# Split weights of the second layer stored for the second sequence, and stores issued one chunk later

## The chip, the cores and the metric

One Trainium2 chip, one core of it. The time is device microseconds (us) of one execution; a time is the median of the runs shown. The profile is one further execution of the same program, and all rows below are from it.

## What is computed

Two independent sequences (`x_prompt`, `x_sample`), each of 16 meta tokens and 512 tokens (528 columns, `T`), go through the same two layers with the same weights:

```
def _trunk(x, ...):
    h = concatenate([meta, x], axis=1)
    h = h + gdn_mixer(rmsnorm(h, ln_g[0]), gdn_w_in, ..., gdn_w_out)     # layer 1
    h = h + mla_mixer(rmsnorm(h, ln_g[1]), mla_w_in, mla_w_uq, mla_w_ukv, ..., mla_w_out)   # layer 2
    return h[:, 16:]
```

Layer 1 is a gated DeltaNet in both directions (8 heads); layer 2 is attention over low-rank projections (16 heads): `cq` and `ckv` are normed projections of the layer's input, q comes from `cq @ w_uq`, k and v from `ckv @ w_ukv`, a rotary part is added, and softmax(q k) v is multiplied by silu of a gate z and projected by `mla_w_out`.

## The kernel before

**Products in two halves.** Every float32 factor x of a projection is kept as a high half `xh` (x cast to float32r) and a low half `xl` = x - `xh`, and a product is three matmuls (`mm3`, L75 to L77): high by high, high by low, low by high. A weight matrix is used in chunks of 4 blocks of 128 rows and 128 columns (256 KB; `wh` and `wl` are the halves of a chunk). Some chunks of layer 2 have 2 blocks and 128 columns (128 KB).

**`weights()`** (L204) prepares chunks. It loads the raw chunk into `wraw` (SP issues the DMA, L218), ScalarE (ACT) casts it into `wh` (L219), and GpSimd (POOL) subtracts, `wl = wraw - wh` (L220, recorded as L88). Each of `wraw`, `wh` and `wl` has three buffers. With `s=0` the two halves are also stored to device memory (`wc`, L222 to L224), and with `s=1` nothing is split: SP loads both halves from `wc` (L211 to L213). Before the change only layer 1 passes `s`: its 98 chunks are split and stored with the first sequence and loaded with the second. The 94 chunks that layer 2 uses of `mla_w_in`, `mla_w_uq` and `mla_w_ukv` are split anew for each sequence, and so are the output projections' chunks, which are used by one sequence at a time and pass no `s`.

**Stages.** `run()` (L1129) emits layer 1 for the first sequence, layer 1 for the second, and then layer 2 in the same way. The output projections (`out_proj`) and the preparations of the next stage (`l2_prep`) are woven in. Layer 2 works on pairs of heads, 8 pairs a sequence. A pair's head (`head(u)`) takes ten chunks in this order: `pair_k` (two, k of both heads), `pair_qrope` (one, the rotary part of q), `pair_q` (one, first head), `pair_v` (one), `pair_q` (second head), `pair_z` (two for each head). It runs beside the attention (`pair_scores`, `pair_out`) of the pair before it.

**The chain inside a pair.** `pair_k` makes the scales of k: `rk` goes out to device memory (`rkd`, L998) and comes back on all partitions as `rs` (L955, 528 KB). `pair_qrope` projects and sends `qg` to `sw` with its quarters swapped, in four DMAs (`swap`, L840, shown as `acc<-acc`). POOL then multiplies (L956, L957), VectorE (DVE) adds (L964) and makes the low half `RL` of the rotary part (two instructions, L970), ACT its high half `SQ` (L968, then a DMA to the other partitions, L969). In the attention DVE takes the maximum `mx` of a score tile (L1089), ACT the exponential into `P` (L1093), DVE scales `P` (L1096), and TensorE (PE) transposes it (L1108, L1110) and multiplies by v. The 0.5 KB rows of `pst` (L1113, L1114) are the meta tokens' share. The gated output of a head, `zs`, is written to `y2` (L1127).

**What sets the order.** Each engine runs its own list of instructions in order. The lists come from the Tile scheduler, which orders the traced instructions by a simulated timeline and puts in the semaphores; `behind()` forces a few orders. All DMAs are issued by SP, one list as well: a DMA whose wait isn't over holds up those behind it.

Of the kernel before, what the change touches and what calls it, by code (L numbers as in the profile page):

```python
# [8 lines left out]
F32 = mybir.dt.float32  # L9
# [14 lines left out]
class Trunk:  # L24
    def __init__(self, ctx, tc, ins, outs):
        self.tc, self.nc, self.ins, self.outs = tc, tc.nc, ins, outs
        self.ctx = ctx
        self.cn = ctx.enter_context(tc.tile_pool(name="cn", bufs=1))
        self.dr = ctx.enter_context(tc.tile_pool(name="dr", space=DRAM, bufs=1))
        self.sa = ctx.enter_context(tc.tile_pool(name="sa", bufs=1, reuse_waits="tile"))  # L30
        self.n = 0
        self.inner = None
        self.cached = {}
        self.last_sc = self.last_P = None
        self.next_pool(self.BUFS1, self.PBUFS1)

# [167 lines left out]
    def weights(self, parts, kt, width=128, hk=4, s=None):  # L204
        nc = self.nc
        res = []
        key = None if s is None else (parts[0][1].tensor.name, parts[0][1].offset)
        for k0 in range(0, kt, hk):
            wh = self.t("wh", [128, hk, width], F32R)
            wl = self.t("wl", [128, hk, width], F32R)  # L210
            if s == 1:  # L211
                for t, c in zip((wh, wl), self.cached[key, k0]):
                    nc.sync.dma_start(t.rearrange("p k c -> p (k c)").bitcast(F32), c)  # L213
            else:
                raw = self.t("wraw", [128, hk, width])
                for off, ap in parts:
                    w = ap.shape[1]
                    nc.sync.dma_start(raw[:, :, off:off + w], ap[128 * k0:128 * (k0 + hk)].rearrange("(k p) c -> p k c", p=128))  # L218
                nc.scalar.copy(wh, raw)  # L219
                self.last_wl = self.sub(nc.gpsimd, wl, raw, wh)  # L220
                if s == 0:
                    self.cached[key, k0] = cs = [self.d("wc", [128, hk * width]) for _ in range(2)]  # L222
                    for t, c in zip((wh, wl), cs):
                        nc.sync.dma_start(c, t.rearrange("p k c -> p (k c)").bitcast(F32))  # L224
            for k in range(hk):
                res.append((wh[:, k], wl[:, k]))
        return res

    def project(self, w, rhs, kt, c0, n, tag="pj", m=128):
        ps = self.p(tag, [m, n])  # L230
# [617 lines left out]
    def l2_prep(self, s, hd, rsd, out):  # L848
        nc = self.nc
        V, A, G, PE = nc.vector, nc.scalar, nc.gpsimd, nc.tensor  # L850
        W = self.ins["mla_w_in"][0]
# [13 lines left out]
        ckv = oh, ol = self.t("ckvH", [128, 2, T], F32R), self.t("ckvL", [128, 2, T], F32R)  # L865
        pss = [self.p(t, [128, 264]) for t in ("x", "tr")]
        for j in range(2):
            w = self.weights([(0, W[:, 512 + 128 * j:640 + 128 * j])], 8)
            for c, c0 in enumerate(KC):
                cs = slice(c0, c0 + 264)  # L870
                ps = self.project(w, hn, 8, c0, 264)
                A.copy(oh[:, j, cs], ps)
                self.sub(V, ol[:, j, cs], ps, oh[:, j, cs])
                sq = self.t("raw", [128, 264])
                A.activation(sq, ps, AF.Square)
                self.colsum(pss[c], self.split("sq", sq, [128, 264]), 0, 264, j == 0, j == 1)
# [8 lines left out]
            A.copy(oh[:, j], x)  # L885
            self.sub(V, ol[:, j], x, oh[:, j])
        yield
        w = self.weights([(0, W[:, 768:832]), (64, W[:, 768:832])], 8)
        kpg = self.t("acc", [128, T])
        sqpe = self.t("raw", [64, T])  # L890
        for c0 in KC:
# [15 lines left out]
        cq = self.t("cqH", [128, 4, 512], F32R), self.t("cqL", [128, 4, 512], F32R)  # L907
        sm = self.t("sqr", [128, 512])
        for j in range(4):
            w = self.weights([(0, W[:, 128 * j:128 * j + 128])], 8)  # L910
            ps = self.project(w, hn, 8, NM, 512)
            gj = self.cqg[:, j:j + 1]
            A.activation(cq[0][:, j], ps, AF.Copy, scale=gj)
# [27 lines left out]
    def pair_qrope(self, u):  # L941
        nc = self.nc
        V, A, G, PE = nc.vector, nc.scalar, nc.gpsimd, nc.tensor
        UQ, cq, hs = self.ins["mla_w_uq"][0], u["c"]["cq"], u["hs"]
        w = self.weights([(64 * j, UQ[:, 192 * h + 128:192 * h + 192]) for j, h in enumerate(hs)], 4)
        ps = self.project(w, cq, 4, 0, 512)
        qg = self.t("acc", [128, 512])
        A.activation(qg, ps, AF.Copy, scale=self.qrg)
# [24 lines left out]
    def pair_k(self, u):  # L973
        nc = self.nc
# [5 lines left out]
        kk = self.t("sqH", [128, T])  # L980
        sq = self.t("raw", [128, T])
        for j, h in enumerate(hs):
            w = self.weights([(0, UKV[:, 256 * h:256 * h + 128])], 2, hk=2)
            for c0 in KC:
                ps = self.project(w, ckv, 2, c0, 264)
                A.copy(kr[:, j, c0:c0 + 264], ps)
            o, nn = self.SIDES[j]
            A.activation(kk[o], kr[nn, j], AF.Square)
            A.activation(sq[o], kr[o, j], AF.Square)
            G.tensor_tensor(kk[o], kk[o], sq[o], op=ALU.add)  # L990
# [9 lines left out]
    def pair_q(self, u, j):  # L1000
# [1 line left out]
        V, A, G, PE = nc.vector, nc.scalar, nc.gpsimd, nc.tensor  # L1002
        UQ, cq, sqr, h = self.ins["mla_w_uq"][0], u["c"]["cq"], u["sqr"], u["hs"][j]
        o = self.SIDES[j][0]
        w = self.weights([(0, UQ[:, 192 * h:192 * h + 128])], 4)
        ps = self.project(w, cq, 4, 0, 512)
        qH = self.t("qH", [128, 512], F32R)
        qL = self.t("qL", [128, 512], F32R)
# [18 lines left out]
    def pair_v(self, u):  # L1027
        nc = self.nc
        V, A, G, PE = nc.vector, nc.scalar, nc.gpsimd, nc.tensor
        UKV, ckv, hs, hp = self.ins["mla_w_ukv"][0], u["c"]["ckv"], u["hs"], u["hp"]  # L1030
        w = self.weights([(128 * j, UKV[:, 256 * h + 128:256 * h + 256]) for j, h in enumerate(hs)], 2, width=256, hk=2)
        VH, VL = self.V2[hp % 2, 0], self.V2[hp % 2, 1]
        for tp in range(2):
            ps = self.p("pj", [128, 2, 256])
# [29 lines left out]
    def pair_z(self, u, j):  # L1064
        nc = self.nc
        V, A, G, PE = nc.vector, nc.scalar, nc.gpsimd, nc.tensor
        W, hn, h = self.ins["mla_w_in"][0], u["c"]["hn"], u["hs"][j]
        w = self.weights([(0, W[:, 832 + 128 * h:960 + 128 * h])], 8)
        ps = self.project(w, hn, 8, NM, 512)
        zs = u["zs"][j] = self.t("zs", [128, 512])  # L1070
        A.activation(zs, ps, AF.Tanh, scale=0.5)
# [260 lines left out]
```

## Time and profile before

| | |
|---|---|
| time, median of 3 runs | 2630.35 us (2624.48 to 2631.34) |
| profiled execution, its own time | 2632.01 us |
| its span, first to last instruction | 2630.3 us |
| PE busy | 2468.7 us, 94% |
| DVE busy | 1732.9 us, 66% |
| ACT busy | 1408.4 us, 54% |
| POOL busy | 1166.6 us, 44% |
| granted TensorE clock, mean | 0.97 |

Layer 1 takes the first 1340 us or so, layer 2 the rest; its first sequence's attention runs to about 1920 us, the second's preparation and attention from there to about 2390 us, and an output projection ends the program. In rows, the number after `x` is a count, and what stands after `|` or in brackets is idle time of the engine before the instruction with what ended it. A line such as L88 is that of a helper: the names of the tiles tell what is worked on.

### The profile page before, as it was taken

The page shows a single profiled execution, that of the slowest core. Times are in us where ns is not written, and L with a number is a line of the kernel's source. Part 1 is how long each engine was busy: PE and PEld are TensorE (multiplying, and loading weights), DVE is VectorE, ACT ScalarE, POOL GpSimd, SP SyncE. Part 2 cuts the span into 40 slices and gives each one's busy share as a digit, 9 for nine tenths or more (in the row PEclk, how much of TensorE's full clock was granted, in tenths as well). Part 3 has the DMA queues.
Part 4 walks back from the last instruction along what each step waited for, and adds up shares of the span by engine and source line. Part 5 has one row for each costly group of instructions (what it writes and reads, how often), then busy time and mean ns, then how long its engine had stood idle before and what let it go on. Part 6 is the DMA issues. An engine that isn't in the chain of part 4 may idle for free.

```text
span 2630.3 us, 52159 instructions
## 1 busy us (share of the span) xinstructions
PE 2468.7 (94%) x19083; PEld 2212.1 (84%) x19083; DVE 1732.9 (66%) x3915; ACT 1408.4 (54%) x3424; POOL 1166.6 (44%) x1157
## 2 busy tenths in 40 slices
PE   8889999998999999999989889998998989999999
PEld 7878888888888889888989878888887878888787
DVE  6987888777788867786454256667775567666421
ACT  5545655545455554545545365666656556665432
POOL 6544545432433323323445454555535544554343
PEclk9999999988999999999999999999999999999999
DMA  6544545442333354444465422233332223225575
GB/s 206 176 121 136 153 128 164 136 138 86 112 91 90 113 172 138 133 122 144 127 213 167 130 79 71 73 72 83 90 89 74 81 70 69 77 69 153 167 222 148
DMA packets 453216, 321.06 MB, mean 122 GB/s; under 512 B 134812, under 2 KB 364430, under 8 KB 452960
## 3 DMA queue, kind: packets, MB, share of 16 engines
q1 hardware_dynamic: 452960, 317.73, 41.9%
q8 instruction: 150, 2.46, 0.4%
q14 instruction: 106, 0.87, 0.1%
HBM read 216.02 MB, written 92.67 MB: 117 GB/s over the span
## 4 chain that ended last, share of the span: by engine, by line
PE 58%; DVE 20%; DMA 8%; ACT 6%; issue 4%; POOL 2%; SPq 2%; ACTq 0%; POOLq 0%; DVEq 0%
PE pj L75 12%; PE pj L76 12%; PE pj L77 12%; PE ch L692 2%; PE po L710 2%; DVE acc L374 2%; DVE RL L88 2%; DMA acc<-acc 2%; DVE Yt L504 1%; DVE kq L374 1%; PE ch L703 1%; DVE Y L506 1%; PE lv L552 1%; PE tr L1110 1%; DMA T<-Td 1%
## 5 line engine op out<-in xcount | busy, mean ns | idle before, releaser
L88 POOL TENSOR_TENSOR wl<-wraw,wh 128x512 fp32r<-128x512 f32 (+2 forms) x414 | 547.6, 1325 | 708.8 <-ACT wh L219 675.3
L75 PE MATMUL pj<-hnH,wh 128*128 128x264 f32 (+4 forms) x2080 | 632.8, 305 | 18.9 <-ACT wh L219 5.2
L77 PE MATMUL pj<-hnH,wl 128*128 128x264 f32 (+3 forms) x2080 | 627.6, 303 | 2.6 <-POOL wl L88 1.9
L76 PE MATMUL pj<-hnL,wh 128*128 128x264 f32 (+3 forms) x2080 | 625.2, 301 | 0.7 <-DVE hnL L784 0.6
L219 ACT CAST wh<-wraw 128x512 fp32r<-128x512 f32 (+2 forms) x414 | 248.2, 600 | 346.0 <-PE pj L76 195.8
L75 PEld LDWEIGHTS pj<-hnH,wh 128*128 128x128 f32 (+1 forms) x2080 | 398.9, 192 | 37.6 <-ACT wh L219 5.7
L77 PEld LDWEIGHTS pj<-hnH,wl 128*128 128x128 f32 (+1 forms) x2080 | 398.3, 192 | 17.8 <-POOL wl L88 3.3
L76 PEld LDWEIGHTS pj<-hnL,wh 128*128 128x128 f32 (+1 forms) x2080 | 399.0, 192 | 15.8 <-issue 2.5
L76 PE MATMUL pj<-h2L,wh 128*128 128x512 f32 (+1 forms) x544 | 205.5, 378 | 3.2 <-DVE h2L L88 3.1
L77 PE MATMUL pj<-h2H,wl 128*128 128x512 f32 (+1 forms) x544 | 205.8, 379 | 0.0
L75 PE MATMUL pj<-h2H,wh 128*128 128x512 f32 (+1 forms) x544 | 205.4, 379 | 0.3
L1089 DVE TENSOR_REDUCE mx<-S 128x1 f32<-128x528 f32 x128 | 89.9, 703 | 66.3 <-PE S L1086 65.5
L1093 ACT ACTIVATE P<-S,mx,qs 128x528 f32<-128x528 f32 x128 | 101.5, 793 | 46.6 <-DVE mx L1090 42.7
L76 PEld LDWEIGHTS pj<-h2L,wh 128*128 128x128 f32 x544 | 102.5, 188 | 22.4 <-DVE h2L L88 4.4
L732 POOL TENSOR_TENSOR oa<-oa,ot 128x256 f32<-128x256 f32 (+1 forms) x80 | 69.6, 870 | 114.5 <-DVE ot L730 101.2
L75 PEld LDWEIGHTS pj<-h2H,wh 128*128 128x128 f32 x544 | 102.3, 189 | 20.0 <-DVE cqL L916 0.6
L77 PEld LDWEIGHTS pj<-h2H,wl 128*128 128x128 f32 x544 | 102.7, 189 | 18.1
L374 DVE SCALAR_TENSOR_TENSOR acc<-raw,vec,acc 128x528 f32<-128x528 f32 x128 | 112.4, 881 | 6.7 <-ACT acc L372 5.7
L374 DVE SCALAR_TENSOR_TENSOR kq<-raw,vec,kq 128x528 f32<-128x528 f32 x128 | 105.7, 826 | 8.6 <-ACT kq L372 7.6
L793 DVE TENSOR_TENSOR raw<-raw,pj 128x512 f32<-128x512 f32 (+1 forms) x54 | 31.3, 580 | 120.9 <-PE pj L77 120.7
L1116 ACT CAST hnH<-tr 128x512 fp32r<-128x512 f32 x128 | 74.9, 585 | 61.5 <-PE tr L1110 59.6
L88 DVE TENSOR_TENSOR hnH<-tr,hnH 128x512 fp32r<-128x512 f32 x128 | 88.2, 689 | 19.6 <-ACT hnH L1116 16.1
(483 smaller groups left out, 6789.1 us busy)
## 6 DMA issues: line engine op xcount, KB each, us to landing
wraw<-in_gdn_w_in_dram SPq DMA_DIRECT2D x96, 256.0 KB
wc<-wh SPq DMA_DIRECT2D x96, 256.0 KB
wc<-wl SPq DMA_DIRECT2D x96, 256.0 KB
wh<-wc SPq DMA_DIRECT2D x96, 256.0 KB
wl<-wc SPq DMA_DIRECT2D x96, 256.0 KB
wraw<-in_mla_w_in_dram SPq DMA_DIRECT2D x88, 256.0 KB
wraw<-in_gdn_w_out_dram SPq DMA_DIRECT2D x64, 256.0 KB
wraw<-in_mla_w_out_dram SPq DMA_DIRECT2D x64, 256.0 KB
```

Of the source, the lines that this page charges most:

```text
L75: mm(out, ah, bh, start=first, stop=False)
L76: mm(out, ah, bl, start=False, stop=False)
L77: mm(out, al, bh, start=False, stop=last)
L88: return eng.tensor_tensor(out, a, hi, op=ALU.subtract)
L219: nc.scalar.copy(wh, raw)
L374: nc.vector.scalar_tensor_tensor(acc, raw[:, j:j + T], self.convw(j, u), acc, op0=ALU.mult, op1=ALU.add)
L692: PE.matmul(pc[:n, 0], kq[:, 0, sl], S[d], start=True, stop=True)
L710: PE.matmul(po[:n, 0], kq[:, 1, sl], S[d], start=True, stop=True)
L732: G.tensor_tensor(oa[:n, i], oa[:n, i], t, op=ALU.add)
L1089: V.tensor_reduce(mx, Sv, axis=AX.XY, op=ALU.max, negate=True)
L1093: self.last_P = A.activation(P, Sv, AF.Exp, bias=mx, scale=qs[j][:, qt:qt + 1], accum_out=sm)
L1116: A.copy(PTH[:, :, hc], pt)
```

## The change

All eight calls of `weights()` in the preparation and the pairs of layer 2 pass `s`, so the first sequence's 94 chunks are stored after the split (188 more stores, 45 MB by the sizes above) and the second's are loaded as halves: 94 casts on ACT and 94 subtractions on POOL are gone, and where SP issued a load of a raw chunk it issues two, of `wh` and of `wl`. A chunk of the rotary part or of k_pe that came in two pieces now comes in one for each half. The output projections are as before. In both layers a chunk's two stores are no longer traced right behind its own split but behind the next chunk's (`store_split`).

```diff
+        self.unstored = []
...
             if s == 1:
+                self.store_split()
                 for t, c in zip((wh, wl), self.cached[key, k0]):
                     nc.sync.dma_start(t.rearrange("p k c -> p (k c)").bitcast(F32), c)
             else:
...
                 nc.scalar.copy(wh, raw)
                 self.last_wl = self.sub(nc.gpsimd, wl, raw, wh)
+                self.store_split()
                 if s == 0:
-                    self.cached[key, k0] = cs = [self.d("wc", [128, hk * width]) for _ in range(2)]
-                    for t, c in zip((wh, wl), cs):
-                        nc.sync.dma_start(c, t.rearrange("p k c -> p (k c)").bitcast(F32))
+                    cs = self.cached[key, k0] = [self.d("wc", [128, hk * width]) for _ in range(2)]
+                    self.unstored = list(zip((wh, wl), cs))
...
+    def store_split(self):
+        for t, c in self.unstored:
+            self.nc.sync.dma_start(c, t.rearrange("p k c -> p (k c)").bitcast(F32))
+        self.unstored = []
...
-            w = self.weights([(0, W[:, 512 + 128 * j:640 + 128 * j])], 8)
+            w = self.weights([(0, W[:, 512 + 128 * j:640 + 128 * j])], 8, s=s)
...
-        w = self.weights([(0, UQ[:, 192 * h:192 * h + 128])], 4)
+        w = self.weights([(0, UQ[:, 192 * h:192 * h + 128])], 4, s=u["s"])
...
-        w = self.weights([(0, W[:, 832 + 128 * h:960 + 128 * h])], 8)
+        w = self.weights([(0, W[:, 832 + 128 * h:960 + 128 * h])], 8, s=u["s"])
```

The lines of the changed kernel stand 1 to 7 further down (L840 is L847, L955 is L962, L1127 is L1134). In layer 1 the lists of PE and DVE are word for word the same apart from that, and on SP, ACT and POOL about a dozen rows in all trade places with a neighbour. The larger moves are in layer 2.

SP in layer 2, second sequence, from the second chunk of a gate to the reload of `rs` in the seventh pair (`y2` is the store of a head's output, `rkd` that of the scales, `acc<-acc` the four swaps, `rs2` the reload). Before:

```order
L218 DMA wraw_29781<-in_mla_w_in_dram 128x4x128
L218 DMA wraw_29854<-in_mla_w_uq_dram 128x4x128
L218 DMA wraw_29927<-in_mla_w_ukv_dram 128x2x128 x2
L218 DMA wraw_30014<-in_mla_w_uq_dram 128x4x128
L998 DMA rkd288_29663<-rk_29601 88x12x1
L1127 DMA y2271_19091<-zs_29192 128x512
L840 DMA acc_29719<-acc_29715 32x512 x4
L955 DMA rs2_29724<-rkd288_29663 128x1056
```

and now, where `wh_30059` and `wl_30060` are the halves of the first head's q:

```order
L215 DMA wl_29989<-wc434_24655 128x512
L1134 DMA y2271_19091<-zs_29421 128x512
L215 DMA wh_30059<-wc435_24731 128x512
L1005 DMA rkd476_29877<-rk_29819 88x12x1
L847 DMA acc_29930<-acc_29926 32x512 x4
L962 DMA rs2_29935<-rkd476_29877 128x1056
L215 DMA wl_30060<-wc436_24732 128x512
L215 DMA wh_30130<-wc437_24809 128x512
L215 DMA wl_30131<-wc438_24810 128x512
```

The loads of q and v stood ahead of the scales' store; now the high half of q stands ahead of it and behind the store of `y2`, and its low half behind the reload of `rs`. In four of the sequence's eight pairs the low half stands so; in two both halves stand between the scales' store and the swaps, in the first pair two halves of a gate's chunk do, and in one both halves of q stand ahead of all.

POOL at the same place, from the scales to the second `sqr`. Before:

```order
L92 TENSOR_TENSOR rk_29601<-rk_29601,mhalf_73 88x12
L88 TENSOR_TENSOR wl_29853<-wraw_29854,wh_29852 128x512
L88 TENSOR_TENSOR wl_29926<-wraw_29927,wh_29925 128x512
L956 TENSOR_TENSOR acc_29715<-acc_29715,rc_19070 128x512
L957 TENSOR_TENSOR acc_29719<-acc_29719,rsn_19071 128x512
L1058 TENSOR_TENSOR acc_29977<-kpr_25782,rs2_29724 128x528
L88 TENSOR_TENSOR wl_30013<-wraw_30014,wh_30012 128x512
L1058 TENSOR_TENSOR acc_30052<-kpr_25782,rs2_29724 128x528
L88 TENSOR_TENSOR wl_30103<-wraw_30104,wh_30102 128x512
L1014 TENSOR_TENSOR sqr_29717<-sqr_29717,raw_29874 64x512
```

and now:

```order
L93 TENSOR_TENSOR rk_29819<-rk_29819,mhalf_73 88x12
L963 TENSOR_TENSOR acc_29926<-acc_29926,rc_19070 128x512
L964 TENSOR_TENSOR acc_29930<-acc_29930,rsn_19071 128x512
L1065 TENSOR_TENSOR acc_30179<-kpr_26144,rs2_29935 128x528
L1065 TENSOR_TENSOR acc_30252<-kpr_26144,rs2_29935 128x528
L1021 TENSOR_TENSOR sqr_29928<-sqr_29928,raw_30079 64x512
```

The four subtractions are gone, the other six stand in the same order.

SP in layer 2, first sequence, at the same steps of its sixth pair. Before:

```order
L218 DMA wraw_24492<-in_mla_w_ukv_dram 128x2x128 x2
L218 DMA wraw_24579<-in_mla_w_uq_dram 128x4x128
L998 DMA rkd280_24228<-rk_24166 88x12x1
L1127 DMA y2270_19090<-zs_23757 128x512
L840 DMA acc_24284<-acc_24280 32x512 x4
L955 DMA rs2_24289<-rkd280_24228 128x1056
```

and now:

```order
L220 DMA wraw_24144<-in_mla_w_ukv_dram 128x2x128 x2
L233 DMA wc412_23996<-wh_23988 128x512
L233 DMA wc413_23997<-wl_23989 128x512
L220 DMA wraw_24235<-in_mla_w_uq_dram 128x4x128
L1134 DMA y2270_19090<-zs_23365 128x512
L1005 DMA rkd407_23864<-rk_23794 88x12x1
L233 DMA wc414_24073<-wh_24065 128x512
L847 DMA acc_23924<-acc_23920 32x512 x4
L962 DMA rs2_23929<-rkd407_23864 128x1056
L233 DMA wc415_24074<-wl_24066 128x512
```

Stores lie between the loads, and one (the high half of q) right ahead of the swaps.

## Rows read from the trace of the kernel before

**Rows 1.** The page's first part: the span, and each engine's busy time, share and instructions.

```profile
PE 2468.7 (94%) x19083; PEld 2212.1 (84%) x19083; DVE 1732.9 (66%) x3915; ACT 1408.4 (54%) x3424; POOL 1166.6 (44%) x1157
```

**Rows 2.** Stretches of time: length, busy time of each engine in it (with counts), the granted TensorE clock, the mean busy share of the DMA engines, GB/s. Layer 2 of the first sequence, of the second, and two short stretches within the second.

```profile
1480.00:1920.00 440.00, 404.38 (x2624) 360.76 (x2623) 280.08 (x535) 260.96 (x574) 230.09 (x164) 0.98 0.31 81
1920.00:2390.00 470.00, 430.40 (x2795) 384.05 (x2794) 304.90 (x587) 283.28 (x636) 236.92 (x173) 0.97 0.29 77
2010.00:2021.00 11.00, 6.13 (x26) 5.53 (x27) 10.77 (x14) 5.35 (x10) 4.24 (x4) 0.53 0.39 95
2331.00:2335.00 4.00, 4.00 (x23) 3.95 (x22) 3.02 (x7) 0.61 (x2) 0.00 (x0) 0.57 0.02 4
```

**Rows 3.** Who PE waited for from 1920 to 2390 us: us in total, times, longest.

```profile
PE S L1108 <- DVE P L1096: 11.3, 6, 3.4
PE pj L75 <- DVE qL L1012: 10.2, 8, 5.4
PE S L75 <- DVE pst L88: 5.9, 5, 1.4
PE x L75 <- ACT hnH L1116: 3.5, 5, 1.8
PE pj L76 <- DVE h2L L88: 3.1, 3, 1.8
```

**Rows 4.** Groups of instructions from 1920 to 2390 us on POOL, ACT and DVE: forms, count, busy us, mean ns, idle before.

```profile
L88 POOL TENSOR_TENSOR wl<-wraw,wh 128x512 fp32r<-128x512 f32 (+1 forms) x90 | 115.5, 1283 | 173.8 <-ACT wh L219 168.2 <-ACT pst L1114 4.5 <-PE tr L1110 0.8
L219 ACT CAST wh<-wraw 128x512 fp32r<-128x512 f32 (+1 forms) x89 | 51.6, 580 | 56.3 <-PE pj L76 27.7 <-issue 14.6 <-POOL rk L92 4.9
L88 DVE TENSOR_TENSOR RL<-acc,SQ 64x512 fp32r<-64x512 f32 x16 | 21.1, 1318 | 2.6 <-ACT SQ L968 2.4
```

**Rows 5.** The chain that ended last, in order of time, in the seventh pair of the second sequence: start, us, what.

```profile
2314.10 3.90 DMA acc<-acc
...
2324.16 1.65 DVE RL L88
2325.84 1.73 DVE RL L88
2327.80 1.20 DVE P L1096
```

**Rows 6.** DVE and PE there, in order of time.

```profile
2321.01 1.81 DVE L964 TENSOR_TENSOR acc<-acc 128x512 f32<-128x512 f32 x1 [1.19 <-POOL acc L957]
...
2324.09 3.48 DVE L88 TENSOR_TENSOR RL<-acc,SQ 64x512 fp32r<-64x512 f32 x2
...
2329.14 0.27 PE L1108 MATMUL S<-ident,P 128*16 128x128 f32 x1 [3.16 <-DVE P L1096]
```

**Rows 7.** POOL there.

```profile
2322.24 1.74 POOL L88 TENSOR_TENSOR wl<-wraw,wh 128x512 fp32r<-128x512 f32 x1
2323.95 1.31 POOL L1058 TENSOR_TENSOR acc<-kpr,rs 128x528 f32<-128x528 f32 x1
2325.75 1.27 POOL L88 TENSOR_TENSOR wl<-wraw,wh 128x512 fp32r<-128x512 f32 x1 [0.49 <-ACT wh L219]
```

**Rows 8.** Single tiles over the whole program: duration in ns, shortest, median and longest.

```profile
L88 DVE TENSOR_TENSOR RL<-acc,SQ x32: 673/1670/1753, 1505.4 to 2378.2; 64x512 fp32r<-64x512 f32 x32
L1096 DVE TENSOR_SCALAR P<-P,sm x128: 478/495/1522, 1538.6 to 2465.2; 128x528 f32<-128x528 f32 x128
```

**Rows 9.** ACT and PE at a wait for `pst`, same pair.

```profile
2299.98 0.62 ACT L219 CAST wh<-wraw 128x512 fp32r<-128x512 f32 x1
...
2300.77 0.25 ACT L1113 CAST pst<-S 16x128 fp32r<-16x128 f32 x1
...
2301.66 0.39 PE L75 MATMUL S<-kH,qH 128*128 128x264 f32 x1 [1.36 <-DVE pst L88]
```

**Rows 10.** The first pair of the second sequence: SP's reload of `rs`, DVE's and POOL's work behind it.

```profile
2002.49 0.34 SPq L955 DMA_DIRECT2D rs<-rkd  x1
2006.70 6.37 DVE L1055 TENSOR_TENSOR kr<-kr,rs 128x528 f32<-128x528 f32 x2 [4.60 <-DMA rs<-rkd]
2009.55 1.25 POOL L88 TENSOR_TENSOR wl<-wraw,wh 128x512 fp32r<-128x512 f32 x1
```

**Rows 11.** SP in the seventh pair (issue time and time to issue), and PE's first use of the low half of q there.

```profile
2310.83 0.34 SPq L1127 DMA_DIRECT2D y<-zs  x1
...
2315.32 0.33 SPq L955 DMA_DIRECT2D rs<-rkd  x1
...
2319.98 0.40 PE L77 MATMUL pj<-cqH,wl 128*128 128x512 f32 x1
```

**Rows 12.** Layer 1: a stretch of the first sequence (split and stored) and one of the second (loaded), columns as in Rows 2.

```profile
200.00:560.00 360.00, 349.56 (x3215) 315.80 (x3214) 284.31 (x713) 203.88 (x555) 178.14 (x216) 0.97 0.50 151
700.00:1190.00 490.00, 479.51 (x4651) 432.74 (x4650) 385.18 (x1060) 247.16 (x704) 147.36 (x212) 0.99 0.42 121
```

**Rows 13.** Layer 1: one load of a low half on SP, and PE's wait for it.

```profile
680.18 0.37 SPq L213 DMA_DIRECT2D wl<-wc  x1
...
682.96 0.39 PE L77 MATMUL pj<-hnH,wl 128*128 128x256 f32 x1 [0.58 <-DMA wl<-wc]
```

**Rows 14.** Layer 1: time to issue a store (ns, shortest, median, longest).

```profile
L224 SPq DMA_DIRECT2D wc<-wh x98: 319/340/969, 13.5 to 558.4; - x98
```

**Rows 15.** What SP itself waited for from 1920 to 2390 us: us in total, times, longest.

```profile
SPq L1127 <- DVE sm L1094: 15.9, 6, 5.0
SPq L1127 <- DVE zs L1125: 15.3, 7, 3.5
```

More of the change, by code (lines that the diff above doesn't have):

```diff
@@ L887, in l2_prep @@
         yield
-        w = self.weights([(0, W[:, 768:832]), (64, W[:, 768:832])], 8)
+        w = self.weights([(0, W[:, 768:832]), (64, W[:, 768:832])], 8, s=s)
         kpg = self.t("acc", [128, T])
@@ L909, in l2_prep @@
         for j in range(4):
-            w = self.weights([(0, W[:, 128 * j:128 * j + 128])], 8)
+            w = self.weights([(0, W[:, 128 * j:128 * j + 128])], 8, s=s)
             ps = self.project(w, hn, 8, NM, 512)
@@ L944, in pair_qrope @@
         UQ, cq, hs = self.ins["mla_w_uq"][0], u["c"]["cq"], u["hs"]
-        w = self.weights([(64 * j, UQ[:, 192 * h + 128:192 * h + 192]) for j, h in enumerate(hs)], 4)
+        w = self.weights([(64 * j, UQ[:, 192 * h + 128:192 * h + 192]) for j, h in enumerate(hs)], 4, s=u["s"])
         ps = self.project(w, cq, 4, 0, 512)
@@ L982, in pair_k @@
         for j, h in enumerate(hs):
-            w = self.weights([(0, UKV[:, 256 * h:256 * h + 128])], 2, hk=2)
+            w = self.weights([(0, UKV[:, 256 * h:256 * h + 128])], 2, hk=2, s=u["s"])
             for c0 in KC:
@@ L1030, in pair_v @@
         UKV, ckv, hs, hp = self.ins["mla_w_ukv"][0], u["c"]["ckv"], u["hs"], u["hp"]
-        w = self.weights([(128 * j, UKV[:, 256 * h + 128:256 * h + 256]) for j, h in enumerate(hs)], 2, width=256, hk=2)
+        w = self.weights([(128 * j, UKV[:, 256 * h + 128:256 * h + 256]) for j, h in enumerate(hs)], 2, width=256, hk=2, s=u["s"])
         VH, VL = self.V2[hp % 2, 0], self.V2[hp % 2, 1]
```

## Prediction

> **What bounds the kernel now.** I read the page's engine shares first: PE is busy for 94% of the span, DVE 66%, ACT 54%, POOL 44% [rows 1]. So the casts and subtractions that go are work of the two least loaded engines, and nothing is won by their sum. In the stretch that the change empties (layer 2 of the second sequence, 1920 to 2390 us) PE is busy 430.4 of 470 us at a granted clock of 0.97 [rows 2]. What can be won there is the 39.6 us without a matmul, and the 0.03 x 470 = 14 us that the clock takes. The first needs the list of whom PE waited for: DVE's scaled `P` 11.3 us, `qL` 10.2, `pst` 5.9, `hnH` 3.5, `h2L` 3.1 [rows 3], together 34. None of them names `wh` or `wl`: the split weights themselves come in time. The gain has to come indirectly, through what the split does to DVE and ACT in the middle of PE's waits.
>
> **What goes, and what it is worth.** 94 subtractions at 1283 ns are 121 us of POOL, 94 casts at 580 ns are 55 us of ACT [rows 4], all beside PE's work. Their worth is read in one wait after another.
>
> *P, 11.3 us.* In the seventh pair the chain runs from the swaps over `RL` (1.65 and 1.73 us) to `P` (1.20) [rows 5]. DVE does L964 in 1.81 us and two `RL` in 3.48, and only then `P`, for which PE waits 3.16 [rows 6]. POOL is in `wl` or L1058 nearly all that time [rows 7]. Over the whole program an `RL` takes 673 ns at the shortest and 1670 in the median, a `P` 478 and 495, but up to 1522 [rows 8]: the same work takes 2.5 times as long beside POOL. Without the `wl`, DVE saves 1.1 us on L964 (taken at the shortest `RL`, whose operation it is on 128 instead of 64 partitions), 2 x 1.0 on `RL` and 0.7 on `P`, if L1058 does not slide into their place: 3.8 us, more than the wait of 3.16. `P` would end at 2325.2 instead of 2329.0. L1058 stays and will hit one of them, so I take about 0.7 of the group: 8 of 11.3. Bounds: 0 (L1058 hits all) and 11.3.
>
> A rule of the Trainium skill fits this ("SBUF — State Buffer", section "Who interferes with whom"): a DVE instruction with two inputs in SBUF contends with a GpSimd instruction that reads SBUF, and the one that comes second is held for the whole of the other. The rows agree as far as the two durations go; by the rule alone the 16 `RL` would give 16 x (1318 - 673) = 10.3 us of DVE, where the sum takes 8 of PE's wait, since L1058 reads SBUF too.
>
> *qL, 10.2 us.* Its longest piece, 5.4, is the first pair's: DVE's `kr` waits 4.60 us for the reload of `rs`, then two take 6.37 with a `wl` on POOL beside them [rows 10]. The reload is a transfer that the change doesn't shorten; the stretch of `kr` is. I take 2.5 of 10.2; bounds 0 and 6.
>
> *pst, 5.9 us.* A cast of 0.62 us stands on ACT right ahead of the `pst` that PE then waits 1.36 for [rows 9]. Gone in five places: 5 x 0.6 = 3; bounds 0 and 5.
>
> *hnH, h2L and the rest.* 6.6 us named; the same two causes, half of it: 3. Sum 8 + 2.5 + 3 + 3 = 16.5.
>
> *Clock.* Granted 0.53 from 2010 to 2021 and 0.57 from 2331 to 2335, near the lower level of 1.2 GHz [rows 2]; both stand right behind a wait of some 3 to 5 us [rows 6, 10]. A dip such as the second costs 0.43 x 4 = 1.7 us. Two of them gone: 3.4; bounds 0 and 14. Gain in all: 20.
>
> **What is added.** Second sequence: 188 loads. In layer 1 a load of a half, issued at 680.18, was used by PE at 682.96, so it takes about 2.8 us, issue included [rows 13]. DMA engines are 0.29 busy here, against 0.42 in layer 1's loaded stretch [rows 2, 12], so bandwidth is no limit. The order in SP's list is. In four pairs the low half of q stands behind the reload of `rs`, and its use is fixed: in the seventh pair the reload is issued at 2315.32 and PE uses the half first at 2319.98, 4.66 later [rows 11]. In the first pair `rs` lands 4.2 us behind its issue (2002.49 to 2006.70) [rows 10]; if the half behind it, sharing the engines with 528 KB, lands 0.7 later, that is 4.9: PE waits 0.2, or up to 1.2 where the reload is late. Taken 0.6 x 4 = 2.5. In the first pair two halves of a gate's chunk stand ahead of the swaps: two issues of 0.33 and some transfer, 1. In five other pairs a load or two stands ahead of the swaps, which head the chain [rows 5]: 0.5 x 5 = 2.5. Together 6; bounds 0 (all inside PE's backlog) and 28 (rival two).
>
> First sequence, layer 2: 188 stores of 0.34 us issue [rows 14] on a SP that has time. In the order shown one lies ahead of the swaps in the sixth pair; 0.34 and a little of transfer, 0.5 for each of 8 pairs, half of it on the path: 2. DMA rises from 0.31 [rows 2] by at most what 45 MB are over 440 us, some 100 GB/s on top of 81, and layer 1 did 151 GB/s at 0.50 with PE 97% busy [rows 12]. Bounds 0 and 8.
>
> Deferred stores, layer 1: PE's and DVE's lists are unchanged, and PE is 349.56 of 360 busy in the stretch that stores [rows 12]. A buffer is held for one chunk longer, of three. Taken 0, bounds -3 and 3.
>
> Sum: -20 + 6 + 2 = **-12**.
>
> **A second way to the same number.** Layer 1 has done this already. Its split stretch has PE idle for 10.4 of 360 us (2.9%), its loaded one for 10.5 of 490 (2.1%) [rows 12]: 0.8% of 470 us is 4, and the clock's 0.97 against 0.99 up to 9 more. So 4 to 13 gained, net of the loads. The stretches differ in work, so it is a support and not a measurement.
>
> **Rivals.** *One, nothing moves (2632, chance 0.25).* The waits of [rows 3] are then dependencies: `P` waits for L964 and for the order of DVE's list, L1058 slides under the `RL` in the place of `wl`, and what is won at one wait is lost at the next. For it: POOL and ACT are the engines with most room [rows 1], and no wait names a weight. Against it: 673 against 1670 ns [rows 8] on the chain itself. The Trainium skill would side with it ("Perfetto Trace Analysis", section "Identifying the Most-Contended Engine"): it says to optimize the engine of the highest occupancy first, and that is PE, of which the change removes nothing.
>
> *Two, slower (2644, chance 0.15).* One mechanism: SP's list. The store of `y2` waits for DVE (31.2 us in 13 waits, 2.4 each, up to 5.0) [rows 15], and it now stands ahead of the high half of q and the scales' store, where before it stood behind them; everything after it, swaps and reload too, comes later. If each of the 8 pairs loses 3.5 us that way (2.4 of the store's wait and 1.1 for the half behind the reload), that is 28, against a gain of 16: +12. It decides from 2 us a pair. Against it: in the seventh pair the store goes at 2310.83, 4.5 us ahead of the reload [rows 11], and POOL and DVE, being freer, let `zs` and the scales come earlier as well.
>
> *Three, the full gain (2600, chance 0.12).* All of `P`, `pst` and half of the rest go (11 + 5 + 6), nearly all of the clock's 14 comes back, less 4 for the loads: -32.
>
> That the second sequence loads what the first stored is plain from the lists; that its first loads find their stores unfinished is excluded by some 400 us between the two.
>
> **How the numbers follow.** Forecast: 2632.0 - 12 = 2620.0 in the profiled execution, whose own time stands 1.7 us above the median, so 2618 for the median, with its own range of 2610 to 2628. Chance 0.48; rival one 0.25, two 0.15, three 0.12. A measurement of this kernel can tell about 0.3%, 7.9 us: faster is below 2622.5, slower above 2638.2. Faster: 0.37 of the 0.48 and 0.12 of rival three and 0.02 of one, 0.51. Slower: 0.12 of rival two and 0.03 of one, 0.15. The rest, 0.34, is the same. The range reaches from three's time, which leaves out half of it, to just short of two's: 2600 to 2640.
>
> **What would show it.** In layer 2 of the second sequence POOL should fall from 237 us by about 120 and ACT from 283 by 52. Right, if `RL` there has a mean near 0.8 us (now 1.32), PE's wait for `P` comes to 3 to 4 us in sum, and that for `pst` is halved. The first sequence's layer 2 should keep its length within 3 us, and layer 1 too. Wrong by rival one, if `RL` is short and PE's idle time is still about 40 us; by rival two, if PE's waits then name `wl` or `wh` of q, or `SQ` and `RL` come later after the pair's begin, behind a waiting `y2`. Wrong in another way, if layer 1 changes: then the longer hold of the buffers costs what I put at nothing.

## The result, and the profile after

The changed kernel takes 2648.70 us (median of 4, 2643.45 to 2653.09) against 2630.22: a ratio of 1.0063, 95% interval 1.0042 to 1.0084. It is slower, by 17 us by the ratio, where 12 less had been forecast.

First the page's engine line of the changed kernel, which answers to [rows 1], and the stretches that answer to [rows 2], which begin at the same distance from the first pair of a sequence and end at the same distance from its eighth (the same columns).

```profile
PE 2487.8 (94%) x19083; PEld 2226.9 (84%) x19083; DVE 1711.4 (65%) x3915; ACT 1364.2 (51%) x3330; POOL 1039.4 (39%) x1063
```

```profile
1487.00:1936.00 449.00, 410.85 (x2607) 366.42 (x2607) 274.44 (x533) 257.94 (x568) 224.33 (x161) 0.95 0.58 162
1938.00:2410.00 472.00, 432.18 (x2768) 383.14 (x2767) 285.59 (x582) 239.27 (x542) 123.40 (x83) 0.96 0.42 122
```

The split is gone as it should be: POOL has 127 us less in all, ACT 44. But the stretch that stores is 449 instead of 440 us at a clock of 0.95 instead of 0.98, and the one that loads is 472 instead of 470, with 39.8 us in which PE has no matmul (472 - 432.2), where it had 39.6. Whom PE waited for in the second of them, which answers to [rows 3] (us, times, longest):

```profile
PE pj L78 <- DMA wl<-wc: 10.7, 5, 3.2
PE S L76 <- DVE pst L89: 6.1, 6, 1.9
PE S L1092 <- DVE kst L89: 4.6, 1, 4.6
PE pj L76 <- DMA wh<-wc: 2.7, 2, 2.2
PE pj L76 <- DVE zs L1079: 2.4, 1, 2.4
...
PE pj L76 <- DVE qL L1019: 1.9, 3, 1.5
```

`P` has left the head of the list and `qL` fell from 10.2 to 1.9; the halves of q took their place. The group of `RL` there, against 1318 ns in [rows 4]:

```profile
L89 DVE TENSOR_TENSOR RL<-acc,SQ 64x512 fp32r<-64x512 f32 x16 | 19.6, 1224 | 0.4
```

So `RL` hardly became shorter. What happens around the swaps is seen in the sixth pair of the first sequence, in order of time, SP and POOL. Before:

```profile
1766.36 0.32 SPq L998 DMA_DIRECT2D rkd<-rk  x1
...
1768.14 2.45 SPq L840 DMA_DIRECT2D acc<-acc  x4
...
1772.97 0.33 SPq L955 DMA_DIRECT2D rs<-rkd  x1
...
1773.80 1.29 POOL L956 TENSOR_TENSOR acc<-acc,rc 128x512 f32<-128x512 f32 x1 [1.96 <-DMA acc<-acc]
```

and after:

```profile
1782.07 0.30 SPq L1005 DMA_DIRECT2D rkd<-rk  x1
1783.26 0.33 SPq L233 DMA_DIRECT2D wc<-wh  x1
...
1783.85 2.45 SPq L847 DMA_DIRECT2D acc<-acc  x4
...
1788.64 0.33 SPq L962 DMA_DIRECT2D rs<-rkd  x1
...
1790.62 1.30 POOL L963 TENSOR_TENSOR acc<-acc,rc 128x512 f32<-128x512 f32 x1 [3.06 <-DMA acc<-acc]
```

From the first swap's issue to the multiplication it was 5.66 us, now 6.77; one store of 256 KB stands between the scales' store and the swaps. The DMA view of the 3 us that begin 1 us after the first swap's issue shows what the engines did: packets and what they moved, and the queue's share of the 16 engines' time in its last column. Before (1769.1 to 1772.1) and after (1784.8 to 1787.8):

```profile
DMA packets 192, 0.26 MB, mean 87 GB/s; under 512 B 64, under 2 KB 64, under 8 KB 192
...
q1 hardware_dynamic: 192, 0.26, 35.6%
```

```profile
DMA packets 45, 0.07 MB, mean 24 GB/s; under 512 B 10, under 2 KB 10, under 8 KB 45
...
q1 hardware_dynamic: 45, 0.07, 96.0%
```

After the change the engines are 96% busy and move 24 GB/s: the 45 packets that begin there take 1.0 us each in the mean (0.96 x 48 us of engine time over 45), where they took 0.09. Ahead of them lies the scales' store, 88 x 12 floats that go out as 1056 packets of 4 bytes.

In the second sequence, where loads stand near, it looks otherwise. Its seventh pair, SP and POOL:

```profile
2334.48 0.38 SPq L1005 DMA_DIRECT2D rkd<-rk  x1
2335.06 2.45 SPq L847 DMA_DIRECT2D acc<-acc  x4
2342.00 0.33 SPq L962 DMA_DIRECT2D rs<-rkd  x1
2342.82 1.29 POOL L963 TENSOR_TENSOR acc<-acc,rc 128x512 f32<-128x512 f32 x1 [8.76 <-DMA acc<-acc]
```

and the DMA view from 2338.7 to 2342.4:

```profile
DMA packets 0, 0.00 MB, mean 0 GB/s; under 512 B 0, under 2 KB 0, under 8 KB 0
```

No packet begins in these 3.7 us, and still POOL waits for the swaps and SP for the scales: here the packets are through, and it is the word of their landing that comes late.

### The profile page after: what moved, and what is told of

Read it like the earlier page. It is cut to its first block, busy times and chain, and to the rows that moved or that the text cites. A ratio compares the mean times of both kernels' runs of the same rounds, so it can differ in the third digit from the quotient of the medians.

```text
span 2649.4 us, 52408 instructions
## 1 busy us (share of the span) xinstructions
PE 2487.8 (94%) x19083; PEld 2226.9 (84%) x19083; DVE 1711.4 (65%) x3915; ACT 1364.2 (51%) x3330; POOL 1039.4 (39%) x1063
## 4 chain that ended last, share of the span: by engine, by line
PE 58%; DVE 18%; DMA 10%; ACT 6%; issue 3%; POOL 3%; SPq 2%; POOLq 0%; ACTq 0%; DVEq 0%
PE pj L76 12%; PE pj L78 12%; PE pj L77 11%; DMA acc<-acc 2%; PE ch L699 2%; DVE acc L381 2%; PE po L717 2%; DVE Yt L511 1%; DVE kq L381 1%; PE tr L1117 1%; PE ch L710 1%; DVE Y L513 1%; DVE RL L89 1%; DMA rkd<-rk 1%; PE lv L559 1%
## 5 line engine op out<-in xcount | busy, mean ns | idle before, releaser
L89 POOL TENSOR_TENSOR wl<-wraw,wh 128x512 fp32r<-128x512 f32 (+2 forms) x320 | 419.6, 1313 | 535.1 <-ACT wh L221 479.3
L221 ACT CAST wh<-wraw 128x512 fp32r<-128x512 f32 (+2 forms) x320 | 193.5, 606 | 288.3 <-PE pj L77 183.8
```

What stands on the lines that cost most here:

```text
L89: return eng.tensor_tensor(out, a, hi, op=ALU.subtract)
```

## The experiments

All ratios are to the kernel before on the same chip, with their interval. "Pairs" are the lengths, in the profiled execution, from the first instruction on the scales (`rk` on DVE) of a sequence's first pair to that of its eighth; "multiplication" is the mean time from the end of `qg` on ACT to POOL's first multiplication (both waits for the swaps and what POOL does before lie in it) in the second to eighth pair.

| kernel | ratio | pairs, first / second sequence | multiplication, first / second |
|---|---|---|---|
| before | 1 | 391.8 / 370.1 | 6.1 / 5.9 |
| changed | 1.0063 (1.0042 to 1.0084) | 401.1 / 372.7 | 7.0 / 8.2 |
| layer1_deferral_only | 0.9996 (0.9980 to 1.0012) | 391.1 / 369.8 | 6.0 / 5.8 |
| stored_not_loaded | 1.0065 (1.0043 to 1.0087) | 402.8 / 365.1 | 7.1 / 5.4 |
| stores_at_once | 1.0082 (1.0053 to 1.0111) | 403.2 / 374.4 | 7.2 / 8.3 |
| loaded_not_stored | 1.0010 (0.9990 to 1.0030) | 396.0 / 371.9 | 6.5 / 8.6 |
| q_ahead_of_reload | 1.0119 (1.0092 to 1.0147) | 400.5 / 385.0 | 7.1 / 10.0 |
| q_and_stores_behind_swaps | 1.0070 (1.0044 to 1.0095) | 407.7 / 369.8 | 6.6 / 7.5 |
| one_store_ahead | 1.0306 (1.0282 to 1.0331) | 427.5 / 408.6 | 10.6 / 10.7 |
| one_store_behind | 1.0041 (1.0021 to 1.0061) | 400.9 / 373.8 | 7.2 / 7.1 |
| swaps_on_act | 1.0168 (1.0140 to 1.0195) | 398.1 / 394.6 | 11.7 / 13.6 |
| far_chunks_only | 0.9977 (0.9958 to 0.9996) | 396.6 / 362.4 | 6.1 / 6.2 |
| coarse_scales_before | 0.9905 (0.9879 to 0.9931) | 380.1 / 354.3 | 4.2 / 4.1 |
| coarse_scales_after | 0.9887 (0.9856 to 0.9918) | 382.2 / 348.8 | 4.2 / 5.0 |
| strided_scales_before | 0.9926 (0.9904 to 0.9947) | 390.3 / 362.7 | 4.3 / 4.2 |
| strided_scales_after | 0.9881 (0.9855 to 0.9907) | 394.4 / 353.3 | 4.3 / 4.7 |
| strided_pairs_only | 0.9895 (0.9867 to 0.9924) | 391.6 / 357.2 | 4.4 / 4.8 |

**The parts of the change.** The deferral alone, put into the kernel before:

```diff
                 self.last_wl = self.sub(nc.gpsimd, wl, raw, wh)
+                self.store_split()
```

> The kernel before with the deferred stores in layer 1 alone; layer 2 splits for both sequences. If the deferral is free, as the prediction had it, the time is that of the kernel before, 2630 within 4 us, and layer 1 ends at the same time. If holding a buffer for one chunk longer costs, the 2 us by which layer 1 of the changed kernel is later at its first unit and the 3 us in the stretch behind its last one show here: 2635.

It is free. The stores without the loads:

```diff
-            if s == 1:
+            if s == 1 and not parts[0][1].tensor.name.count('mla'):
```

> The changed kernel with layer 2's chunks stored in the first sequence and split again in the second (what is stored there is never read). Theory: the 188 stores cost 12 to 15 us in the first sequence's layer 2 (3 in its preparation, 9 in its pairs, mostly as a lower granted clock), so 2643 to 2646. Rival: the longer first sequence comes from another order or from the clock by itself, and the stores are free: 2630 to 2634.

The stores alone cost all of the difference (1.0065 against 1.0063), so the loads are worth nothing in sum, as far as these intervals tell. Their place, at once or one chunk later:

```diff
                 self.last_wl = self.sub(nc.gpsimd, wl, raw, wh)
-                self.store_split()
...
                     self.unstored = list(zip((wh, wl), cs))
+                    self.store_split()
```

> The changed kernel with a chunk's stores issued right behind its own split, in both layers. If the place of the stores doesn't matter, only their bytes and issues, 2645 to 2651 like the changed kernel. If the deferral put them in front of the swaps and that is what costs, the first sequence's layer 2 is 5 to 9 us shorter again and the time 2639 to 2643.

No gain by it; the deferral isn't what costs. And the loads without the stores:

```diff
-                for t, c in zip((wh, wl), self.cached[key, k0]):
+                cs = self.cached.get((key, k0)) or self.big[self.rot % 160:][:2]
+                for t, c in zip((wh, wl), cs):
...
-                if s == 0:
+                if s == 0 and 'mla' not in key[0]:
```

> The changed kernel with no stores in layer 2; the second sequence loads its halves there from what layer 1 stored, so its weights in layer 2 are others, in the same number and sizes. It leaves the first sequence without stores. Theory: the stores cost 15 to 17 us and the loads give nothing in sum, so 2630 to 2636, with the second sequence's pairs as long as in the changed kernel (372 us). Rival: what the loads give is 10 us or more and was lost to what the stores left in the queues: 2618 to 2624.

As expected, the second sequence's pairs are as long as in the changed kernel. The first sequence's, 396.0 without a single store there, show how far one profile's length strays.

**The order on SP.** The first theory was that of places: q's low half behind the reload, stores and loads ahead of the swaps. In the second sequence the reload is moved into `pair_q`, behind the first head's loads:

```diff
-        with self.tc.issue_after(last.ins):
+            with self.tc.issue_after((self.last_ld if u["s"] else last).ins):
...
+        if u["s"] and j == 0:
+            u["reload"]()
```

> The changed kernel with the reload of rs forced behind both halves of the first head's q in the second sequence (all else as it is). Theory: PE's waits for the low half of q (10.2 us in four pairs) and the dips of the clock right behind them (four of 1.7) go, and the rest stays: 2632 to 2638. Rival: the half that comes earlier makes the reload later and the chain of the scales takes the wait over: 2645 to 2650, with PE waiting for kst or kL instead of wl.

It failed, and not only by the rival: in three pairs the reload now stood ahead of the swaps, which were issued 4 to 6 us late. A wider edit forces the order of the stores, of the loads of the first head's q (`hold`), and of the reload behind both:

```diff
+            with self.behind(self.last_sw):
+                self.nc.sync.dma_start(c, t.rearrange("p k c -> p (k c)").bitcast(F32))
...
+                    with self.behind(self.last_sw if hold else None):
...
+            with self.behind(last, self.last_ld if u["s"] else None):
```

> The changed kernel with three orders forced on SP's list: a store of a half traced behind a pair's swaps is issued behind them, in the second sequence both halves of the first head's q are issued behind the swaps, and the reload of rs behind those. Theory: the swaps then land as in the kernel before, the first sequence's pairs fall from 401 to some 392 us, the second's from 372 to 355 to 362, and the time is 2622 to 2632. Rival: what is held back comes too late itself (q's halves for PE, or the reload for kr): 2640 to 2650, with PE waiting for wh, wl or kst.

PE's waits in the first sequence's pairs, and one of ACT's:

```profile
PE pj L77 <- ACT wh L223: 14.3, 7, 4.2
...
PE S L1125 <- DVE P L1113: 1.7, 5, 0.6
ACT wh L223 <- DMA wc<-wh: 34.9, 6, 8.6
```

The rival was right: the held stores held the buffers, ACT's casts waited 34.9 us for them, and PE waited for the split. The wait for `P` fell to 1.7 us (12.2 in the changed kernel's pairs), but that doesn't show that the swaps made it: the multiplication comes only 0.4 us earlier than in the changed kernel (6.6 against 7.0), and the kernel before, with 6.1, waits 11.0 us for `P` in these pairs.

One store more in each pair of the kernel before, ahead of the swaps (`put` is the scales' store, `first` the first swap) and behind them:

```diff
+        with self.tc.issue_after(u["put"].ins):
+            one = nc.sync.dma_start(c, whole)
+        with self.tc.issue_after(one.ins):
+            first = nc.sync.dma_start(sw[0:32, 0:512], qg[32:64, 0:512])
```

```diff
+        with self.tc.issue_after(last.ins):
+            nc.sync.dma_start(c, whole)
```

> The kernel before, splitting as before, with one extra store of 256 KB in each of the 16 pairs (the high half of the rotary chunk, to a place that nothing reads), issued between the scales' store and the four swaps. Theory: a transfer right ahead of the swaps holds them up by its own length, as it stands in the traces of the changed kernel (POOL's first multiplication 7.4 to 7.6 us behind qg where a store precedes, 5.5 to 6.1 where none does), and a pair then loses 1 to 1.3 us, waits and clock together: 16 to 20 us, so 2646 to 2650. Rival: the delay is hidden, and the stores cost through their number and bytes: 16 of 188, 1 to 2 us, so 2630 to 2633.

> The same 16 stores, each issued right behind the last of the four swaps. Theory (the place counts): POOL's multiplication at 5.5 to 6.5 us behind qg and 2630 to 2636 in all. Rival (the bytes count, wherever they stand): the same time as with the store ahead.

Sixteen stores ahead cost 3.1%, four to five times what was expected, and behind 0.4%, more than expected. A store ahead begins 0.37 us after the scales' store (SP, ACT and POOL, a pair of the first sequence):

```profile
1797.07 0.32 SPq L1006 DMA_DIRECT2D rkd<-rk  x1
1797.44 0.61 SPq L957 DMA_DIRECT2D one<-wh  x1
1798.10 0.55 SPq L959 DMA_DIRECT2D acc<-acc  x1
...
1804.88 1.66 ACT L220 CAST wh<-wraw 128x512 fp32r<-128x512 f32 x3 [5.35 <-DMA one<-wh]
1805.58 2.54 POOL L88 TENSOR_TENSOR wl<-wraw,wh 128x512 fp32r<-128x512 f32 x2 [8.53 <-ACT wh L220]
1808.07 1.30 POOL L964 TENSOR_TENSOR acc<-acc,rc 128x512 f32<-128x512 f32 x1
```

It is 10 us from the first swap to the multiplication, but the swaps aren't all of it. Right ahead of the multiplication, without a pause, POOL does two subtractions; they wait for a cast, and the cast waits until the added store has left its buffer, 7.4 us after its issue. In each of the second to sixteenth pairs POOL comes out of two subtractions so. The 10.6 us of the table and the 3.1% hold this wait for a buffer, which the changed kernel doesn't have (no cast waits for a store in its pairs), and the run doesn't give the price of a store near the swaps by itself.

In the changed kernel's sixth pair the store follows the scales' by 1.2 us, the swaps by 1.8, and the multiplication comes about 1 us later than before. In its fifth and seventh pairs the store stands nearer still, 0.6 us behind the scales', but the swaps begin 3.2 behind them, and the multiplication comes 5.9 and 6.1 us behind `qg`, where it was 6.1 and 5.7 before. So a store between the scales' and the swaps doesn't set the price by its bytes or its place alone; what is different in the pairs that pay is that the swaps follow the scales closely. That made the second theory: the scales' own packets.

The swaps of q taken off SP; with them goes the reload's order behind them:

```diff
-            last = self.nc.sync.dma_start(dst[a:a + 32, 0:c], src[b:b + 32, 0:c])
+            last = (self.nc.scalar if queue else self.nc.sync).dma_start(dst[a:a + 32, 0:c], src[b:b + 32, 0:c])
...
-        last = self.swap(sw, qg, 512)
+        self.swap(sw, qg, 512, queue=True)
...
-        with self.tc.issue_after(last.ins):
+        if True:
```

> The changed kernel with the four swaps issued by ACT right behind qg instead of by SP. Theory (the delay is that of one queue): the swaps pass the stores and loads, POOL's multiplication comes at 5 to 6 us behind qg, PE's waits for P shrink by half in the first sequence, against some 2.5 us of issue a pair on ACT: 2632 to 2642. Rival (the delay is in the engines that all queues share, or ACT's issues cost as much): 2645 or more.

The time is the rival's, but neither of its two causes is shown by itself. ACT's four issues take about 2.2 us in most pairs, as had been taken, but ACT then stands between them. In a pair of the second sequence the third and fourth are one row:

```profile
2225.86 6.85 ACTq L847 DMA_DIRECT2D acc<-acc  x2
```

The two issues in it take 0.60 and 0.51 us; the 5.7 us between them are ACT's queue waiting for an earlier load of `wh` to land.

The 11.7 and 13.6 us of the table are not the swaps' landing: in all of these pairs L1065, which waits for the reload, now stands ahead of the multiplication on POOL. Only in the sixth pair of the first sequence are the swaps what POOL waits for last:

```profile
1780.38 1.33 POOL L1065 TENSOR_TENSOR acc<-kpr,rs 128x528 f32<-128x528 f32 x1 [1.33 <-DMA rs<-rkd]
1782.14 1.29 POOL L963 TENSOR_TENSOR acc<-acc,rc 128x512 f32<-128x512 f32 x1 [0.44 <-DMA acc<-acc]
```

The Trainium skill says in "DMA: Bandwidth & Descriptors", section "Issuing engines are not separate DMA queues", that DMAs end on the same 16 engines, whichever engine issues them. This pair agrees: the multiplication comes 10.7 us behind `qg`, where it was 6.8 in the changed kernel. Of that ACT's queue stood 2.9 us between the second swap and the third, until the scales had landed; and the fourth landed 5.2 us after its issue had ended, where it was 4.3, so the swaps did not pass.

**The scales in larger pieces.** The second theory, in one line:

```diff
-        nc.sync.dma_start(rkd.rearrange("j (i p) -> p j i", p=88), rk)
+        nc.sync.dma_start(rkd.rearrange("j (p i) -> p j i", p=88), rk)
```

> The changed kernel with the scales' store in 176 pieces of 24 bytes instead of 1056 of 4 (the tokens' scales come back in another order, so the scaled k is another; the amount of work is the same). In the traces a store's packets right behind the 4-byte ones take 0.5 to 1.5 us each, and the swaps stand behind them. Theory: it is these tiny packets that hold the store; then POOL's first multiplication comes at 6 instead of 7 us behind qg in the first sequence and the time falls by 6 to 10 us against the changed kernel. Rival: a store stalls there by itself or by its bytes: no more than 2 us.

> The same edit in the kernel before, as its control: no store stands near the scales but y2 in four pairs. By the theory 0 to 4 us faster, from the earlier reload alone.

Both are about 1% faster than the kernel before, and the changed kernel is 1.8% faster than without the edit (0.9887 / 1.0063). In the kernel before nothing else moved: the lists of all engines are the same, row by row, so its 1.0% is that of 176 pieces instead of 1056. It was put at 0 to 4 us and is 25: the small pieces cost most where no store stands near. In the changed kernel the lists of PE, DVE and ACT in the first sequence's pairs are the same too, and there the stores now cost 2.1 us (382.2 against 380.1) instead of 9.3. In the second sequence the scheduler also changed the order: in none of the eight pairs does the low half of the first head's q stand behind the reload any more, and PE's 10.7 us of waits for `wl` are gone. What the pieces and what this order gave there isn't separated. The theory is right in kind and much too small in size. The same with the tokens in their order:

```diff
-            PE.matmul(ps[:, i], kk[:, 88 * i:88 * i + 88], self.two, start=True, stop=True)
+            PE.matmul(ps[:, i], kk[:, i:T:6], self.two, start=True, stop=True)
```

> The kernel before with the scales' column sums taken over every sixth token, so that a partition holds six tokens in a row and the scales go out in 176 pieces of 24 bytes in their right order. Nothing is left out. If the strided weight load costs PE nothing that shows, the time is that of coarse_scales_before, 0.99 of the kernel before; if it does, some us more.

> The changed kernel with the same edit. Theory: without the 4-byte pieces the change is what its own terms make it: the pairs of the first sequence lose 2 us, those of the second gain 5 to 6, the preparation loses some 5 by its stores; so within 5 us of strided_scales_before, 0.987 to 0.992 of the kernel before. Rival: the gain in coarse_scales_after came from the permuted order, and the changed kernel stays 10 us or more behind.

The same pair of the first sequence in strided_scales_after, and its DMA view from 1781.9 to 1784.9:

```profile
1779.05 0.30 SPq L1005 DMA_DIRECT2D rkd<-rk  x1
1780.30 0.33 SPq L233 DMA_DIRECT2D wc<-wh  x1
...
1780.89 2.45 SPq L847 DMA_DIRECT2D acc<-acc  x4
...
1784.89 1.29 POOL L963 TENSOR_TENSOR acc<-acc,rc 128x512 f32<-128x512 f32 x1 [0.29 <-DMA acc<-acc]
```

```profile
DMA packets 213, 0.34 MB, mean 114 GB/s; under 512 B 66, under 2 KB 66, under 8 KB 213
...
q1 hardware_dynamic: 213, 0.34, 43.8%
```

The issues stand at the same distances as in the changed kernel's pair, the store ahead of the swaps too; the multiplication comes 4.0 us behind the first swap instead of 6.77, and the reload, which waits for the scales, 4.4 us behind their issue instead of 6.6. Here, too, the lists of PE, DVE and ACT in the first sequence's pairs are those of the changed kernel, and those of the second sequence are not. The changed kernel is now the faster: 0.9881 / 0.9926 = 0.9955, 12 us, and by the two intervals together 0.34% either way. In the coarse pair it is 0.9887 / 0.9905 = 0.9982, within what the two intervals allow of no difference.

Two versions that store less:

> The changed kernel with only those chunks of layer 2 stored and loaded whose transfers lie away from the swaps: v, the second head's q and the first head's gate (four of a pair's ten chunks; the preparation's none). Theory: the swaps stand free in both sequences, so the first sequence costs 1 to 4 us and the second gains 3 to 8: 2622 to 2630 where the kernel before has 2630. Rival (any store costs by its bytes, 64 of 188): 5 us slower.

> strided_scales_after with the preparation's 14 chunks split in both sequences, only the pairs' 80 stored and loaded. If the longer preparation of the first sequence (331 to 338 us against 325 to 328) comes from its 28 stores, 4 to 6 us less than strided_scales_after and less than strided_scales_before; if it comes from the clock by itself, no difference.

The first is a small gain without touching the scales, at the edge of its interval, with a first sequence that the profile doesn't show shorter. The second (0.9895) isn't better than strided_scales_after: the longer preparation isn't shown to come from its stores. strided_scales_after has the lowest ratio of the kernels here that compute all of it; the intervals don't tell it from strided_pairs_only.

## Why the prediction was wrong

**The step that failed** is the price of a transfer near the swaps: "0.34 and a little of transfer, 0.5 for each of 8 pairs" for the stores, and "0.5 x 5" for the loads. The multiplication came 0.9 us later in the mean of the first sequence's pairs and 2.3 in the second's, and the first sequence's pairs lost 9.3 us where 2 were taken. What the prediction has nowhere is the scales' store in 4-byte pieces ahead of the swaps: with 24-byte pieces, and the lists of PE, DVE and ACT there unchanged, the same stores cost 2.1 us (coarse) and 4.1 us (strided). Most of the 9.3 us is clock. Of the 9 us between 440 [rows 2] and 449, PE's time without a matmul has 2.5 (35.6 to 38.2) and its busy time 6.5, at a granted clock of 0.95 instead of 0.98; the waits grew little in sum, but three instead of one of the pairs' were over 3 us, and behind those the clock stood at its lower level for some us, as from 1577 to 1583, right behind a wait of 3.14 us for `hnH`:

```profile
1577.00:1583.00 6.00, 5.09 (x24) 4.88 (x24) 5.87 (x13) 3.36 (x8) 1.89 (x2) 0.50 0.36 115
1584.00:1600.00 16.00, 16.00 (x103) 14.21 (x102) 10.79 (x23) 9.90 (x23) 7.44 (x6) 1.00 0.51 159
```

The rows ahead of the prediction had one warning, the swaps' 3.90 us [rows 5], and I took the DMA engines' 0.29 to mean room. A mean share says nothing of a few us in which they are held.

**q's low half** was costed at 0.6 in four pairs, from the reload's 4.66 us lead over its use [rows 11]. It is 10.7 us in five waits, 2.1 each. In the seventh pair now:

```profile
2342.00 0.33 SPq L962 DMA_DIRECT2D rs<-rkd  x1
2342.43 0.38 SPq L215 DMA_DIRECT2D wl<-wc  x1
...
2347.21 0.50 PE L78 MATMUL pj<-cqH,wl 128*128 128x512 f32 x1 [1.79 <-DMA wl<-wc]
```

It landed 5.2 us behind the reload's issue, near the 4.9 worked out, but PE wanted it 3.4 behind (5.21 - 1.79), not 4.66: the use wasn't fixed against the reload, which waits for the scales (24.4 us in seven of this sequence's pairs, 15.0 before) and slid back.

**The first pair's two halves ahead of the swaps** were put at 1 us. PE waited 4.64 there for `kst`, and the clock was 0.53 from 2037 to 2048: the same price as the wait of 5.4 for `qL` and its dip had before [rows 2, 3], so nothing was gained where 2.5 had been taken.

**What was right.** The deferral costs nothing. The wait for `qL` went, even more than taken, and that for `P` too (1.6 us in the pairs, 10.8 before), though not by a shorter `RL`: 1224 ns, since L1065 slid into the place of `wl`, as rival one had it; what shortened it stays open. `pst` stayed at 6.1 where half was to go. So most of the gain at the waits came, and the loads took it back: 6 us had been taken for them, and the waits for `wl`, `kst` and `wh` alone are 18 (10.7 + 4.6 + 2.7). Where the scales are no longer in 4-byte pieces, the result comes nearer to the terms: the first sequence's pairs lose 2 and 4 us by the stores (taken 2), the second's gain 5.5 and 9.4, order and loads together, where 14 net had been taken, and the whole is 12 us faster in the strided pair; the coarse pair's 5 us are within its intervals. That the strided pair's 12 is also the forecast's number is partly luck. Of the rivals, the second had the sign, nearly the size (+12) and its own mark, PE waiting for `wl` and `wh` of q. Its mechanism isn't what the trace shows: in every pair the scales' store leaves SP within 0.6 us of POOL's last work on the scales, and the first swap within 0.4 us of `qg`, so no waiting `y2` holds them.

**Open** is why what stands behind the scales' store is late, and whether the number of the pieces or their size does it; the edit changed both. It may be two things: in the sixth pair of the first sequence packets are held, in the seventh of the second no packet is under way and the landing is told late. In the second sequence the swaps also follow the scales more closely than before (by 0.6 us or less in five of eight pairs, where it was 1.2 to 3.2), so that the loads made the multiplication later there isn't shown. And not all of the loss is located: of the 19 us between the two profiled spans 9.3 lie in the first sequence's pairs and 2.6 in the second's, but 7.4 ahead of the first pair, which begins anywhere from 1470 to 1490 us in these runs, also where nothing is stored up to there in layer 2.

## What to carry to other kernels

Before a transfer is added, look what stands next to it in the DMA engines and not only at their mean share: a store of many tiny pieces stood ahead of packets that took 1.0 us each instead of 0.09. On a chain that goes through device memory, the size of the pieces is worth an experiment before any order of the queues is. And when an added transfer turns a saving into a loss, measure the saving's two halves apart, as stored_not_loaded and loaded_not_stored did, before the order is argued. An added transfer also holds the buffer that it reads: look on every engine for who waits for it, before a delay is put down to the queue.

## What the runs showed of the hardware

A 4 KB store in each of 16 pairs cost this kernel 1.0% by going out in 1056 pieces of 4 bytes: with 176 pieces of 24 bytes, and all lists the same, POOL's multiplication behind the swaps came 1.8 to 1.9 us earlier a pair, and the kernel before fell to 0.9905. The Trainium skill, "DMA: Bandwidth & Descriptors", section "Specifications", puts transfers below 512 B under line rate, since they are read and rewritten. The runs agree that such a store is long in landing (6.6 us from its issue to the reload that waits for it, 4.4 or less with 24-byte pieces); that it is read and rewritten, no run here shows. Larger transfers issued 1.2 and 1.8 us behind it were slow as well (96% busy at 24 GB/s, 44% at 114 GB/s with 24-byte pieces). A weight load of every sixth column took 248 ns instead of 158 (L993 in strided_scales_before; 158 is the median in the kernel before):

```profile
L993 PEld LDWEIGHTS pj<-two,sqH x192: 227/248/249, 1484.5 to 2360.8; 128*88 128x88 f32 x192
```

which is 192 x 90 ns = 17 us of weight loads. Whether they are why strided_scales_before gains less than coarse_scales_before isn't shown: 0.9926 and 0.9905 lie within each other's intervals.
